# Hybrid encoder block on one Trainium2 core: four stage boundaries reordered, and a PSUM bank for each up product

## Chip, core and metric

The kernel runs on one NeuronCore of a Trainium2 chip. The metric is device time in microseconds from the start to the end of one execution; the time before is 1674.95 us, the median of 3 runs (1673.62 to 1676.17). Engines are named as the profile names them: PE is TensorE, DVE is VectorE, ACT is ScalarE, POOL is GpSimd, SP is the engine whose queue issues the DMAs.

## What is computed

One layer of a hybrid encoder on x of 1024 rows by 1024 columns, all in float32. Cut to what matters here:

```python
h = rmsnorm(x, norm_mix_g)
c_q, c_kv, k_rope, mq, mk, mv, mo, mgates, gate_a, gate_b = split_cols(h @ w_in)
y_attn = mla_branch(c_q, c_kv, k_rope, cos, sin, ...)   # latents c_q, c_kv; rotary tables cos, sin
y_mlstm = mlstm_branch(mq, mk, mv, mo, mgates, ...)
merged = sigmoid(gate_a) * (y_attn @ w_branch_mla) + sigmoid(gate_b) * (y_mlstm @ w_branch_mlstm)
x = x + merged @ w_out
u = rmsnorm(x, norm_mlp_g) @ w_mlp_up                   # 1024 -> 4096
x = x + square(relu(u)) @ w_mlp_down                    # 4096 -> 1024
return rmsnorm(x, norm_final_g)
```

## The kernel before

**Precision by splitting.** Nearly every operand of a product is held as two fp32r tiles, a rounded high part and the rest. `split` (line 77) makes them: a cast on ACT (line 79), then a subtraction on DVE (line 80), which waits for the cast. A product of two operands is three matmuls (high by high, high by low, low by high). Activations scaled in the split go through lines 82 and 83.

**Buffers.** All working tiles of 4 KB a partition come from one pool of 46 slots. Raw weights come from a second pool of 4 (`wr`). PSUM has two double banks (`bankA`) and four single ones (`bankB`). A tile waits until a buffer of its pool is free, which is when the last reader of an earlier tile is done.

**What sets the order.** The program is unrolled and traced. A planner of the tile framework then gives each engine its own list of instructions: it goes by modelled durations, takes what is ready and has a buffer, and prefers what comes earlier in the program. On the chip each engine's list runs in that order, with semaphores between the engines. DMA issues stand in SP's list in the same way.

**Gate b and the latents.** `gate_b` (line 823) has eight steps. Step m takes 128 gate columns (`w_ga`, prefetched one entry ahead), a tanh on ACT (line 829), a scaling on DVE (line 830), then 128 columns of the mLSTM branch product, multiplies the two on DVE (line 836) and stores the result. At its end it calls `down_sums` (line 794): two 512 KB loads of down weights, four DVE operations (lines 801 to 804), two 512 KB stores. Those sums serve the down product much later. After gate b come `rotary` (line 396: angle steps on DVE, lines 407 to 419, one Sin on ACT, line 420, copies on DVE) and `latents` (line 857), whose first act is `w_la.get("cq")`. That fetches the query latent's weights in four chunks of 128x768, and the next three chunks as well, and splits them. `Stream.fetch(upto)` (line 114) loads and splits the entries up to a given one that are not yet split.

**Up.** The up product is done in 16 pairs of 128-column blocks with Strassen-like sums: seven products of 512 columns a pair, each of 12 matmuls (`product`, line 1160). They are named by their two operands: 11x11, 12x21, S2xT2, S3xT3, S1xT1, 22xT4, S4x22. `Pair.load` requests raw up weights (line 1122), `plain` splits the block for "11" and "12", `sums`, `sums_14` and `plain_22` make the rest. The right-hand operands T1 to T4 and 22 are made once, by `minus` (line 1288) and `parts` (line 1281), in the stretch between the output product and `up_pair`. In that same stretch the first two products of pairs 0 to 4 are done early (`first_products`, line 1172; its copies to SBUF on ACT are lines 1177 and 1179). `up_pair` (line 1197) does the other five of those pairs, and all seven of pairs 5 to 15. `add` (line 1198) adds a bank to an SBUF tile on DVE. In `up_pair`, before the change, bank `b1` holds 11x11 plus 12x21; `b2` accumulates S2xT2, then S3xT3, then 22xT4, and is read by an `add` after each; `b3` accumulates S1xT1, then S4x22. After its products `activate` runs relu and square on ACT (lines 1184, 1185), and `keep` does four more DVE operations (lines 1190 to 1193) and stores seven 256 KB tiles to DRAM (`hid_d`).

**Down.** `operands(p, ph)` (line 1350) loads and splits two pairs of tiles of up pair p for phase ph: hidden tiles and down weights, 512 KB each, through the four `wr` buffers (line 1334), casts at line 79 and subtractions at line 80 as `dh` and `dl`. The first group of the down product takes operands of pairs 0 to 3, one pair after the other (`dmul`, line 1370; matmuls at lines 1376 to 1378); the next phase's operands are requested after the first half of the products.

Of the kernel before, what the change touches and what calls it, by code (L numbers as in the profile page):

```python
# [38 lines left out]
def kernel(ctx: ExitStack, tc: tile.TileContext, x, positions, norm_mix_g, w_in, mla_q_norm_g,  # L39
# [16 lines left out]
    def nm(p):  # L56
        cnt[0] += 1
        return f"{p}{cnt[0]}"

    def slot(shape, dt=F32, p="s"):  # L60
        return sl.tile(shape, dt, tag="s", name=nm(p))
# [4 lines left out]
    def bankA(p="a"):  # L66
        return psa.tile([P, 1024], F32, tag="A", name=nm(p))

    def bankB(p="b"):
        return psb.tile([P, 512], F32, tag="B", name=nm(p))  # L70
# [16 lines left out]
    class Stream:  # L87
# [5 lines left out]
        def add(self, key, w, cols, K):  # L93

            N = sum(n for _, n in cols)
            per = max(1, 1024 // N)
            for k0 in range(0, K // P, per):
                kn = min(per, K // P - k0)
                self.plan.append((key, [w[k0 * P:(k0 + kn) * P, c:c + n] for c, n in cols], kn, N))
            self.where[key] = len(self.plan)  # L100
# [137 lines left out]
    w_ml, w_ga, w_la, w_at, w_mg = Stream(2), Stream(1), Stream(3), Stream(0), Stream()  # L238
# [555 lines left out]
    def down_sums(p):  # L794

        y, z = slot([P, 2, 512], F32, "wy"), slot([P, 2, 512], F32, "wz")
        rows = w_mlp_down[0][2 * p * P:(2 * p + 2) * P, :].rearrange("(j p) n -> p j n", p=P)
        nc.sync.dma_start(out=y, in_=rows[:, :, 0:512])
        nc.sync.dma_start(out=z, in_=rows[:, :, 512:1024])
        a, b = slot([P, 2, 512], F32, "wt"), slot([P, 2, 512], F32, "wt")  # L800
        nc.vector.tensor_tensor(out=b[:, 1], in0=z[:, 0], in1=y[:, 0], op=ALU.subtract)
        nc.vector.tensor_tensor(out=a[:, 0], in0=z[:, 1], in1=b[:, 1], op=ALU.subtract)
        nc.vector.tensor_tensor(out=a[:, 1], in0=z[:, 1], in1=z[:, 0], op=ALU.subtract)
        nc.vector.tensor_tensor(out=b[:, 0], in0=y[:, 1], in1=a[:, 0], op=ALU.subtract)
        nc.sync.dma_start(out=wd_d[p][:, 0:2, :], in_=a)
        nc.sync.dma_start(out=wd_d[p][:, 2:4, :], in_=b)

    summed = list(range(DFF // P // 2))
# [14 lines left out]
    def gate_b():  # L823
        for m in range(8):
            wt = w_ga.get(("gb", m))
            pa = bankA()
            yield from tr_mm(pa, xT, wt)
            s = slot([P, 1024], F32, "sg")
            nc.scalar.activation(out=s, in_=pa, func=AF.Tanh, scale=0.5)
            nc.vector.tensor_scalar(out=s, in0=s, scalar1=0.5, scalar2=0.5, op0=ALU.mult, op1=ALU.add)  # L830
            if m == 0:
                yield from flip_y()
            wt = w_ga.get(("wb", m))
            pa = bankA()
            yield from tr_mm(pa, yT_tr, wt)
            nc.vector.tensor_tensor(out=s, in0=pa, in1=s, op=ALU.mult)
            dt_ = dr.tile([P, 1024], F32, tag="brb", name=nm("db"), bufs=8)
            nc.sync.dma_start(out=dt_, in_=s)
            brb.append(dt_)
            dump("brb", s, lambda o, m=m: o[m])  # L840
            down_sums(summed.pop(0))


    up = {}
# [308 lines left out]
    NP = DFF // P // 2  # L1153
    pairs = [Pair(p) for p in range(NP)]
# [5 lines left out]
    def product(o, p, a, b, first):  # L1160

        ah, al = pairs[p].ops[a]
        for k in range(4):
            bh, bl = B[b][k // 2]
            bh, bl = bh[:, k % 2], bl[:, k % 2]
            for i, (x_, y_) in enumerate(((ah, bh), (ah, bl), (al, bh))):
                nc.tensor.matmul(out=o, lhsT=x_[:, k], rhs=y_, start=(first and k == 0 and i == 0),  # L1167
                                 stop=(k == 3 and i == 2), skip_group_check=True)
# [28 lines left out]
    def up_pair(p):  # L1197
        add = lambda o, x_, y_: nc.vector.tensor_tensor(out=o, in0=x_, in1=y_, op=ALU.add)
        nx = pairs[p + 1] if p + 1 < NP else None
        if p + 2 < NP:  # L1200
            pairs[p + 2].load()
        r0, b1 = early.pop(p, None), None
        if r0 is None:
            b1 = bankB()
            r0 = slot([P, 2, 512], F32, "r")
            product(b1, p, "11", "11", True)
            nc.scalar.copy(out=r0[:, 1], in_=b1)
        m1 = r0[:, 1]
        u = slot([P, 2, 512], F32, "u")
        b2 = bankB()  # L1210
        product(b2, p, "S2", "T2", True)
        add(u[:, 0], b2, m1)
        if b1 is not None:
            product(b1, p, "12", "21", False)
            nc.scalar.copy(out=r0[:, 0], in_=b1)
        if nx and p + 1 >= EARLY:
            nx.plain()
        product(b2, p, "S3", "T3", False)
        add(u[:, 1], b2, m1)
        if nx:  # L1220
            nx.sums()
        r1 = slot([P, 2, 512], F32, "r")
        b3 = bankB()
        product(b3, p, "S1", "T1", True)
        add(r1[:, 1], b3, u[:, 1])
        if nx:
            nx.plain_22()
        product(b2, p, "22", "T4", False)
        add(r1[:, 0], b2, m1)
        activate(r1)  # L1230
        if nx:
            nx.sums_14()
        product(b3, p, "S4", "22", False)
        add(r0[:, 1], b3, u[:, 0])
        activate(r0)
        keep(p, r0, r1, u)
        pairs[p] = None
# [12 lines left out]
    for half in range(2):  # L1250
        xs = []
        for j in range(4):
            t = half * 4 + j
            xx = slot([P, 1024], F32, "xm")
            nc.sync.dma_start(out=xx, in_=x[0, t * P:(t + 1) * P, :])
            pa = bankA()
            for n in range(2):
                nat_mm(pa[:, n * 512:(n + 1) * 512], mg, t, wo[n])
            nc.vector.tensor_tensor(out=xx, in0=pa, in1=xx, op=ALU.add)
            dump("xmid", xx, lambda o, t=t: o[t])  # L1260
            nc.sync.dma_start(out=xmd[t], in_=xx)
            xs.append(xx)
            if half == 1 and j in (1, 3):
                pairs[j // 2].load(1)
                pairs[j // 2].plain()
        for q in range(4):
            f = slot([P, 2, 512], F32, "xf")
            for i in range(2):
                k = 2 * q + i
                pb = bankB()  # L1270
                for j in range(4):
                    nc.tensor.transpose(out=pb[:, j * P:(j + 1) * P], in_=xs[j][:, k * P:(k + 1) * P], identity=ident)
                nc.scalar.activation(out=f[:, i], in_=pb, func=AF.Copy, scale=vec("gmlp", k))
            blk[q // 2, half, q % 2] = f
            if half == 0:
                h, l = slot([P, 2, 512], F32R, "bh"), slot([P, 2, 512], F32R, "bl")
                split(h, l, f)
                B.setdefault(f"{q // 2 + 1}1", []).append((h, l))
        if half == 0:
            squares(half, xs)  # L1280
# [9 lines left out]


    t1 = [minus(blk[0, 1, q], blk[0, 0, q]) for q in range(2)]
    pairs[2].load(1)
    pairs[2].plain()
    t2 = [minus(blk[1, 1, q], t1[q]) for q in range(2)]
    for q in range(2):
        parts("T2", t2[q])
    pairs[0].load()
    for p in range(2):
        early[p] = first_products(p)  # L1300
    pairs[0].sums()
# [1 line left out]
    pairs[0].sums_14()  # L1303
    for q in range(2):
        parts("T3", minus(blk[1, 1, q], blk[0, 1, q]))
    pairs[3].load(1)
    pairs[3].plain()
    early[2] = first_products(2)
    for q in range(2):
        parts("T1", t1[q])  # L1310
    pairs[4].load(1)
    pairs[4].plain()
    early[3] = first_products(3)
    for q in range(2):
# [4 lines left out]
    squares(1, xs)  # L1319
    nc.vector.tensor_scalar(out=rsq, in0=msq, scalar1=EPS, scalar2=None, op0=ALU.add)  # L1320
    nc.vector.reciprocal(out=rsq, in_=rsq)


    pairs[1].load()
    for p in range(NP):
        up_pair(p)


    GD = 4

# [6 lines left out]
    def in_pair(srcs):  # L1337
        r = raw_pair(srcs)
        h, l = slot([P, 2, 512], F32R, "dh"), slot([P, 2, 512], F32R, "dl")
        split(h, l, r)  # L1340
        return [(h[:, j], l[:, j]) for j in range(2)]
# [8 lines left out]
    def operands(p, ph):  # L1350

        if ph == 3:
            return in_last(p)
        right = ([down_row(p, 0)[:, 0:512], down_row(p, 1)[:, 0:512]] if ph == 0 else
                 [wd_d[p][:, 2 * (ph - 1) + j, :] for j in range(2)])
        return [in_pair([hid_d[p][:, 2 * ph + j, :] for j in range(2)]), in_pair(right)]

    acc = {}

# [42 lines left out]
                                       op0=ALU.mult, op1=ALU.add)  # L1402

    NG = NP // GD
    nxt = [operands(p, 0) for p in range(GD)]
    xm = [None] * 8
    every = range(GD)
    for g in range(NG):
# [22 lines left out]
        nxt = [operands(p, 1) for p in group]  # L1431
# [15 lines left out]
        nxt = [operands(p, 2) for p in group]  # L1447
# [5 lines left out]
        if not last:  # L1453
# [9 lines left out]
            nxt = [operands(p + GD, 0) for p in group]  # L1463
# [41 lines left out]
```

## Time and profile before

| What | us |
|---|---|
| median of 3 runs | 1674.95 |
| the profiled execution | 1676.88 |
| its span, first to last instruction | 1675.1 |
| PE busy | 1614.1 |
| DVE busy | 1051.5 |
| ACT busy | 745.0 |

A row of the timeline gives the start and the length in us, the engine, the line of the kernel, the operation, the tile written and the tiles read, shapes and count; in square brackets stands how long the engine had been idle before it and what ended that. A row of the table by stretches gives the stretch, its length, then the busy time of PE, of the weight loads (PEld), of DVE, ACT and POOL with their instruction counts, then the granted share of PE's clock, the busy share of the DMA engines and the GB/s moved. A full clock is 2.4 GHz, a share of 0.50 is 1.2 GHz.

### The profile page before, as it was taken

The numbers are of one execution on the slowest core, as the hardware profiler recorded it, in microseconds if no ns is written. First come the engines' busy times: TensorE is split into PE (matmuls) and PEld (weight loads), VectorE is DVE, ScalarE is ACT, GpSimd is POOL, SyncE is SP. The second block draws the span as 40 slices with busy tenths as digits, with TensorE's granted clock in tenths as the row PEclk, the third lists the DMA queues.
The fourth block names the chain that finished last, engine by engine and source line by source line (L and its number), as shares of the span: only waits on it lengthen the run. The fifth ranks groups of instructions, "written<-read, shape, count | busy, mean of one in ns | idle before, by whom it ended". The sixth has DMA issues, their size and how long they took to land.

```text
span 1675.1 us, 22459 instructions
## 1 busy us (share of the span) xinstructions
PE 1614.1 (96%) x8421; PEld 1358.4 (81%) x8421; DVE 1051.5 (63%) x1551; ACT 745.0 (44%) x1275; POOL 196.0 (12%) x363
## 2 busy tenths in 40 slices
PE   7999999999998999999999998999999989999997
PEld 6789888888887988989888886778888868888885
DVE  5686857665334257787887226666666456666695
ACT  6254444432112267676763125544444356333342
POOL 4021120200000343334310000000000000000001
PEclk9999999999998999999999998999999999999999
DMA  7122220366563000000026532454444377655752
GB/s 217 50 77 64 85 92 14 107 232 204 191 216 123 14 1 14 2 13 1 7 70 251 164 102 76 138 176 170 139 151 140 125 245 246 210 182 192 252 188 101
DMA packets 160528, 211.03 MB, mean 126 GB/s; under 512 B 10835, under 2 KB 93732, under 8 KB 160420
## 3 DMA queue, kind: packets, MB, share of 16 engines
q1 hardware_dynamic: 160388, 209.60, 37.5%
q8 instruction: 66, 1.08, 0.3%
q14 instruction: 42, 0.34, 0.1%
q10 hardware_dynamic: 32, 0.01, 0.0%
HBM read 146.65 MB, written 62.91 MB: 125 GB/s over the span
## 4 chain that ended last, share of the span: by engine, by line
PE 86%; DVE 5%; ACT 3%; issue 3%; POOL 1%; DMA 1%; SPq 0%; POOLq 0%; ACTq 0%; DVEq 0%
PE b L1167 17%; PE a L232 7%; PE a L228 7%; PE a L227 7%; PE a L204 5%; PE a L205 5%; PE a L206 5%; PE b L1007 3%; PE a L1377 3%; PE a L1378 3%; PE a L1376 3%; PE b L1377 2%; PE b L1376 2%; PE b L1378 2%; PE a L986 2%
## 5 line engine op out<-in xcount | busy, mean ns | idle before, releaser
L227 PE MATMUL a<-th,wh 128*128 128x512 f32 x504 | 201.4, 400 | 0.0
L228 PE MATMUL a<-tl,wh 128*128 128x512 f32 x504 | 201.4, 400 | 0.0
L79 ACT CAST dh<-wr 128x1024 fp32r<-128x1024 f32 x112 | 114.2, 1049 | 157.3 <-PE a L1377 49.0
L80 DVE TENSOR_TENSOR dl<-wr,dh 128x1024 fp32r<-128x1024 f32 x112 | 134.1, 1221 | 62.0 <-ACT dh L79 61.3
L1167 PE MATMUL b<-bh,wh 128*128 128x512 f32 x384 | 151.2, 399 | 11.6 <-ACT wh L79 7.1
L232 PE MATMUL a<-th,wl 128*128 128x512 f32 x504 | 162.2, 399 | 0.0
L204 PE MATMUL a<-wh,th 128*128 128x256 f32 (+5 forms) x504 | 161.6, 321 | 0.2 <-ACT mo L569 0.2
L205 PE MATMUL a<-wl,th 128*128 128x256 f32 (+5 forms) x504 | 160.5, 319 | 0.3 <-DVE wl L80 0.3
L206 PE MATMUL a<-wh,tl 128*128 128x256 f32 (+5 forms) x504 | 160.5, 319 | 0.0
L1167 PE MATMUL b<-bl,wh 128*128 128x512 f32 x384 | 152.2, 396 | 0.0
L1167 PE MATMUL b<-bh,wl 128*128 128x512 f32 x384 | 150.7, 396 | 0.0
L306 POOL TENSOR_SCALAR m<-m 128x1 f32<-128x1 f32 (+1 forms) x40 | 9.8, 245 | 1093.1 <-ACT o L1383 802.5
L227 PEld LDWEIGHTS a<-th,wh 128*128 128x128 f32 x504 | 94.7, 188 | 20.6 <-issue 0.2
L228 PEld LDWEIGHTS a<-tl,wh 128*128 128x128 f32 x504 | 94.7, 188 | 20.4
L232 PEld LDWEIGHTS a<-th,wl 128*128 128x128 f32 x504 | 94.0, 188 | 20.8
L1377 PE MATMUL a<-dl,dh 128*128 128x512 f32 x256 | 101.9, 398 | 2.7 <-DVE dl L80 2.7
L80 DVE TENSOR_TENSOR wl<-wr,wh 128x1024 fp32r<-128x1024 f32 (+6 forms) x86 | 93.2, 1096 | 15.8 <-ACT wh L79 11.8
L1378 PE MATMUL a<-dh,dl 128*128 128x512 f32 x256 | 101.5, 397 | 0.0
L204 PEld LDWEIGHTS a<-wh,th 128*128 128x128 f32 x504 | 95.2, 189 | 6.7 <-ACT P L993 0.5
L205 PEld LDWEIGHTS a<-wl,th 128*128 128x128 f32 x504 | 95.2, 189 | 6.4 <-DVE wl L80 0.8
L206 PEld LDWEIGHTS a<-wh,tl 128*128 128x128 f32 x504 | 95.1, 189 | 5.4
L1167 PEld LDWEIGHTS b<-bh,wh 128*128 128x128 f32 x384 | 72.7, 189 | 31.8 <-ACT wh L79 8.5
(310 smaller groups left out, 3727.0 us busy)
## 6 DMA issues: line engine op xcount, KB each, us to landing
wr<-hid SPq DMA_DIRECT2D x112, 256.0 KB, 3.9
wr<-in_w_mlp_up SPq DMA_DIRECT2D x37, 512.0 KB, 4.0
wdd<-wt SPq DMA_DIRECT2D x32, 512.0 KB, 3.1
hid<-r SPq DMA_DIRECT2D x64, 256.0 KB, 2.1
wr<-wdd SPq DMA_DIRECT2D x64, 256.0 KB, 4.4
wr<-in_w_in SPq DMA_DIRECT2D x24, 512.0 KB, 3.8
wr<-in_w_mlp_down SPq DMA_DIRECT2D x48, 256.0 KB, 2.7
wy<-in_w_mlp_down SPq DMA_DIRECT2D x16, 512.0 KB, 5.6
```

Source lines behind the costliest of these rows:

```text
L79: nc.scalar.copy(out=h, in_=src)
L80: (eng or nc.vector).tensor_tensor(out=l, in0=src, in1=h.bitcast(F32), op=ALU.subtract)
L204: nc.tensor.matmul(out=ps, lhsT=xh, rhs=wh, start=(k == 0), stop=False)
L205: nc.tensor.matmul(out=ps, lhsT=xh, rhs=wl, start=False, stop=False)
L206: nc.tensor.matmul(out=ps, lhsT=xl, rhs=wh, start=False, stop=(k == n - 1))
L227: nc.tensor.matmul(out=o, lhsT=wts[k][0], rhs=xh, start=(k == 0), stop=False)
L228: nc.tensor.matmul(out=o, lhsT=wts[k][0], rhs=xl, start=False, stop=False)
L232: nc.tensor.matmul(out=o, lhsT=wts[k][1], rhs=xh, start=False, stop=(k == n - 1))
L1167: nc.tensor.matmul(out=o, lhsT=x_[:, k], rhs=y_, start=(first and k == 0 and i == 0), stop=(k == 3 and i == 2), skip_group_check=True)
L1376: nc.tensor.matmul(out=o, lhsT=ah[:, c], rhs=bh, start=st, stop=False, skip_group_check=True)
L1377: nc.tensor.matmul(out=o, lhsT=ah[:, c], rhs=bl, start=False, stop=False, skip_group_check=True)
L1378: nc.tensor.matmul(out=o, lhsT=al[:, c], rhs=bh, start=False, stop=en, skip_group_check=True)
```

## The change

Four places are edited; what is computed stays the same.

1. In `gate_b` the down-weight sums are made two at a time in steps 1 and 3, one at a time in steps 0, 2, 4 and 5, and not in steps 6 and 7. At the end of step 6 the four chunks of the query latent's weights are fetched, which loads and splits them.
2. Before the up pairs: the raw weights of pairs 2 and 3 are requested at the end of the output product, the split of pair 3 comes before the first products of pairs 0 and 1, and the load of pair 4 comes where pair 3's was.
3. In `up_pair` S3xT3 and 22xT4 each get a bank of their own. The additions on DVE take the sum so far from SBUF in place of the accumulation in PSUM.
4. In the last up pair the operands of down pairs 0 and 1 are requested and split behind the S1xT1 product; those of pairs 2 and 3 stay behind the up pairs. For that the helper functions of the down product move above the loop over the pairs.

```diff
@@ gate_b
-            down_sums(summed.pop(0))
+            for _ in range(2 if m in (1, 3) else 1 if m < 6 else 0):
+                down_sums(summed.pop(0))
+            if m == 6:
+                w_la.fetch(4)
@@ up_pair
-        product(b2, p, "S3", "T3", False)
-        add(u[:, 1], b2, m1)
+        b2 = bankB()
+        product(b2, p, "S3", "T3", True)
+        add(u[:, 1], b2, u[:, 0])
...
         product(b3, p, "S1", "T1", True)
+        if p == NP - 1:
+            nxt.extend(operands(i, 0) for i in range(2))
         add(r1[:, 1], b3, u[:, 1])
...
-        product(b2, p, "22", "T4", False)
-        add(r1[:, 0], b2, m1)
+        b2 = bankB()
+        product(b2, p, "22", "T4", True)
+        add(r1[:, 0], b2, u[:, 1])
@@ between the output product and the up pairs
             if half == 1 and j in (1, 3):
                 pairs[j // 2].load(1)
                 pairs[j // 2].plain()
+            if half == 1 and j == 3:
+                pairs[2].load(1)
+                pairs[3].load(1)
...
 t1 = [minus(blk[0, 1, q], blk[0, 0, q]) for q in range(2)]
-    pairs[2].load(1)
 pairs[2].plain()
...
 pairs[0].load()
+    pairs[3].plain()
 for p in range(2):
     early[p] = first_products(p)
...
-    pairs[3].load(1)
-    pairs[3].plain()
+    pairs[4].load(1)
 early[2] = first_products(2)
...
-    pairs[4].load(1)
 pairs[4].plain()
...
+    nxt = []
 for p in range(NP):
     up_pair(p)
...
-    nxt = [operands(p, 0) for p in range(GD)]
+    nxt += [operands(p, 0) for p in range(2, GD)]
```

## Rows read from the trace of the kernel before

**Rows 1.** The page's first part: busy time, share of the span, instructions.

```profile
PE 1614.1 (96%) x8421; PEld 1358.4 (81%) x8421; DVE 1051.5 (63%) x1551; ACT 745.0 (44%) x1275; POOL 196.0 (12%) x363
```

**Rows 2.** Timeline of PE: the first matmul behind each of its waits.

```profile
516.98 1.33 PE L204 MATMUL b<-wh,th 128*128 128x384 f32 x3 [7.58 <-ACT wh L79]
...
1032.32 1.28 PE L1167 MATMUL b<-bh,wh 128*128 128x512 f32 x2 [7.13 <-ACT wh L79]
...
1069.77 0.50 PE L1167 MATMUL b<-bh,wh 128*128 128x512 f32 x1 [1.13 <-DVE u L1198]
...
1344.90 1.09 PE L1376 MATMUL a<-dh,dh 128*128 128x512 f32 x2 [4.84 <-ACT dh L79]
1347.94 0.80 PE L1377 MATMUL a<-dl,dh 128*128 128x512 f32 x1 [1.96 <-DVE dl L80]
```

**Rows 3.** Table by stretches: behind three waits, one up pair, one gate step.

```profile
516.98:522.50 5.52, 5.52 (x17) 5.34 (x18) 3.62 (x5) 3.06 (x4) 0.00 (x0) 0.50 0.62 193
...
1032.30:1037.90 5.60, 5.58 (x13) 4.33 (x14) 5.58 (x6) 3.29 (x4) 0.00 (x0) 0.50 0.33 94
1347.90:1351.90 4.00, 3.96 (x9) 3.17 (x10) 2.92 (x3) 1.04 (x1) 0.00 (x0) 0.50 0.82 246
1085.60:1101.50 15.90, 14.55 (x60) 11.05 (x60) 11.14 (x17) 6.75 (x7) 0.00 (x0) 1.00 0.54 182
466.60:483.25 16.65, 16.65 (x73) 13.51 (x73) 6.16 (x8) 2.48 (x3) 0.52 (x16) 1.00 0.57 198
```

**Rows 4.** Timeline of DVE, ACT and SP between gate b and the latents.

```profile
515.47 0.29 DVE L419 TENSOR_SCALAR s<-s 128x256 f32<-128x256 f32 x1
...
515.79 0.42 ACT L420 ACTIVATE rot<-s 128x256 f32<-128x256 f32 x1 [9.56 <-DVE s L419]
516.12 3.02 ACT L79 CAST wh<-wr 128x768 fp32r<-128x768 f32 x4
...
497.42 1.64 SPq L110 DMA_DIRECT2D wr<-in_w_in  x1
```

**Rows 5.** Timeline of DVE: the last two weight splits of gate b.

```profile
489.24 1.23 DVE L80 TENSOR_TENSOR wl<-wr,wh 128x1024 fp32r<-128x1024 f32 x1 [0.24 <-ACT wh L79]
...
495.70 0.68 DVE L80 TENSOR_TENSOR wl<-wr,wh 128x512 fp32r<-128x512 f32 x1
```

**Rows 6.** The page's DMA issues: count, KB each, median us to landing.

```profile
wr<-in_w_in SPq DMA_DIRECT2D x24, 512.0 KB, 3.8
```

**Rows 7.** Waits, whole span: engine, line, releaser, total us, times, longest.

```profile
DVE wt L801 <- DMA wz<-in_w_mlp_down: 9.0, 3, 4.5
```

**Rows 8.** Timeline of DVE and ACT before the up pairs.

```profile
1025.56 1.22 DVE L1288 TENSOR_TENSOR xt<-xf,xf 128x1024 f32<-128x1024 f32 x1
...
1031.23 1.04 ACT L79 CAST wh<-wr 128x1024 fp32r<-128x1024 f32 x1
1032.18 0.58 ACT L1177 COPY r<-b 128x512 f32<-128x512 f32 x1
```

**Rows 9.** Timeline of DVE between up pairs 0 and 1.

```profile
1063.59 0.69 DVE L1198 TENSOR_TENSOR r<-b,u 128x512 f32<-128x512 f32 x1 [1.84 <-PE b L1167]
1066.50 0.69 DVE L1190 TENSOR_TENSOR u<-r,r 128x512 f32<-128x512 f32 x1 [2.22 <-ACT r L1185]
...
1069.03 0.68 DVE L1198 TENSOR_TENSOR u<-b,r 128x512 f32<-128x512 f32 x1
```

**Rows 10.** Chain that ended last, merged: pairs 4 to 15 (start, us, what).

```profile
1117.37 222.70 PE b L1167 x960
```

**Rows 11.** Timeline of ACT and SP between up and down.

```profile
1338.04 1.06 ACT L1184 ACTIVATE r<-r 128x1024 f32<-128x1024 f32 x1 [8.23 <-DVE r L1198]
1342.87 3.87 ACT L79 CAST dh<-wr 128x1024 fp32r<-128x1024 f32 x4
1350.17 1.04 ACT L79 CAST dh<-wr 128x1024 fp32r<-128x1024 f32 x1 [3.43 <-DMA wr<-hid]
...
1316.46 0.81 SPq L1334 DMA_DIRECT2D wr<-in_w_mlp_down  x2
```

More of the change, by code (lines that the diff above doesn't have):

```diff
@@ L1321 @@
     nc.vector.reciprocal(out=rsq, in_=rsq)
-    pairs[1].load()
-    for p in range(NP):
-        up_pair(p)
     GD = 4
@@ L1356, in operands @@
         return [in_pair([hid_d[p][:, 2 * ph + j, :] for j in range(2)]), in_pair(right)]
+    pairs[1].load()
+    nxt = []
+    for p in range(NP):
+        up_pair(p)
     acc = {}
```

## The prediction

> **What bounds the kernel now.** I read the page's engine shares first: TensorE (PE) is busy 96% of the span [rows 1]. So an edit pays only where it takes away PE idleness or a stretch in which PE runs at the half clock. I then went through PE's timeline for its waits behind the first 30 us. The long ones stand at the four places that the diff touches [rows 2]: 7.58 us before the first latent product (a cast on ACT ends it), 7.13 us before the up products of pair 3 (again a cast), 1.13 us inside each of pairs 1 to 4 (a DVE addition; one row of four, the others are 1.10 to 1.14), and 4.84 and 1.96 us before the down products (a cast, then the subtraction behind it). Third, the table by stretches shows the clock [rows 3]: after each of the three long waits the granted share is 0.50, that is 1.2 GHz instead of 2.4, for 5.52, 5.58 and 3.96 us of PE work, half of which is lost. After the 1.13 us waits it stays at 1.00.
>
> **Latent weights ahead of the rotary tables.** PE stands still because ACT's queue holds the four latent casts at 516.12 behind the Sin of the rotary table, which waited 9.56 us for DVE's angle steps, the last at 515.47. The weights had long been requested, the last chunk at 497.42 [rows 4]. The change puts the casts and subtractions of all four chunks into the seventh step of gate b. ACT works there 2.48 us of 16.65 and DVE 6.16 [rows 3], so 4 casts of 0.75 (3.02/4) and 4 subtractions of about 0.9 fit beside PE. What would be late next? Not ACT, which still reaches the first square only after Sin at 516.2: 17 matmuls in 5.52 us at half clock are 0.16 each at full clock, a tile of 24 takes 3.9 us, and four banks give PE 15.6 us before it needs a reader. So the 7.58 us go, and with them the half-clock loss of 5.52/2 = 2.76: **10.3 us**.
>
> Two costs stand against this. First, the four latent chunks now stand in the four-buffer weight ring ahead of the last branch weights, whose split ended at 496.4 [rows 5], about 7.5 us before PE began them (24 matmuls of 0.23 before the end at 509.4). Their load must now wait for a latent chunk's subtraction on DVE. If that runs only after the addition at 492.8, the weights are ready around 500 (0.9 subtraction, 3.8 load [rows 6], 1.4 split), so some 4 us are left: nothing. Second, the down-weight sums are doubled in steps 1 and 3. Each adds four DVE operations (2.5 us, so 8.7 of 16.65) and 2 MB to the 3.3 MB that a step moves at 198 GB/s, or 320 GB/s in these two steps. If a load lags, DVE waits in L801 with the next weight split queued behind it. Earlier in the kernel it did so three times, 4.5 us at most [rows 7]. The gate split ends at 490.5 [rows 5], 2.2 us before PE needs it, so the price is 0 to 2 x 2.3 = 4.6 us. I take 0, since loads run a step ahead. Range of this part: 5.7 to 10.3.
>
> **Up weights sooner.** At 1025.2 PE has done "11" of pairs 0 to 2 and "12" of pairs 0 and 1. It then needs pair 3's weights, cast at 1031.23, and "12" of pair 2 needs ACT's copy of its first half, which runs at 1032.18. Both stand in ACT's queue behind the casts of T3, whose first subtraction DVE starts at 1025.56 [rows 8]. Pair 3's cast now comes ahead of pair 0's sums. "11" of pair 3 (12 x 0.232 = 2.78 us) then fills 1025.2 to 1028.0. The copy of pair 2 still stands behind T3, which slips by the 1.2 us of the moved subtraction: to about 1032.4, PE again at 1033.0. That leaves a 5 us gap instead of 7.1, but four products behind it instead of five. The last "12" now ends at 1032.3 + 5 x 2.78 + 2.79 = 1049.0. After the change it is 1033.0 + 4 x 2.78 + 0.3 = 1044.4 if the clock stays, 1047.2 if it falls as now: 1.8 to 4.6 gained. If the copy gets ahead of the T3 casts, all 7.13 + 2.79 = 9.9 can go. I take **4**, near the walk, with 1.8 to 9.9 kept. The load of pair 4 moves too, but its buffer comes free at the same moment (pair 2's subtraction), so it costs nothing. Pair 3's own load moves in the ring ahead of pair 0's two and was long landed: nothing.
>
> **A bank for each up product.** In pairs 0 to 4 PE waits because S3xT3 accumulates into the bank that DVE has still to read, and that addition stands on DVE behind the previous pair's last four operations, which wait 2.22 us for ACT's two activations: addition at 1069.03, 5.4 us after the previous pair's last addition [rows 9]. With 60 matmuls in 15.9 us [rows 3] against 960 in 222.70 [rows 10], or 13.9 per 60, a pair loses 1.95; four such pairs lose 7.8 us. With a bank of its own S3xT3 need not wait. Next late is the last product, which still accumulates on S1xT1's bank. DVE must read that first, and in its queue the read stands behind the sums of the next pair. From one pair's last addition to the next's: 0.7 addition, 2.2 activations, 2.5 for four operations, 1.2 for two additions, 1.8 for three sums, 1.05 cast, 1.2 subtraction, 0.65 read, 2.78 product, an estimated 0.3 of hand-overs: 14.4 us, against PE's 13.9. So 1.45 of 1.95 is gained, four times: **5.8 us**; bounds 3 (half as much) and 7.8. In pairs 5 to 15 PE runs without a gap today [rows 10], so nothing is gained there. Five products now share four banks; the fifth takes the bank of the second, read about 7 us before, so it costs nothing as long as PE keeps program order.
>
> **First down operands sooner.** ACT is idle 8.23 us before 1338.04 while the operands of pairs 0 and 1, requested by 1316.46, wait to be cast at 1342.87 [rows 11]. Cast in that gap, 4 x 0.97 us, they let PE go on when the last up product ends. Costs: their four subtractions (1.2 each) stand on DVE ahead of the read of S1xT1's bank, so the last product starts up to 0.9 later. Pairs 2 and 3 follow only after the last activation (1343) and the last four DVE operations 2.5 us later, while PE ends pairs 0 and 1 by about 1346.5: some 2 us of wait. Loads of the next phase are bounded by four weight buffers; ACT waits for them 3.43 us at 1350.17 [rows 11], so I leave another 1.5. Lost now: 4.84 + 1.96, half of 3.96, half of 1.09 [rows 2, 3], 9.3 in all. Gain 9.3 - 4.4 = **5 us**, bounds 0 and 9.3.
>
> **The sum.** 10.3 + 4 + 5.8 + 5 = 25.1 us. The profiled execution took 1676.88 us, of which 1675.1 is the span; 1676.9 - 25.1 = 1651.8. It lay 1.9 above the median of the runs, so 1650 for the median.
>
> **The rivals.** *The planner keeps the old order.* Each engine's order is set at build by a planner that goes by modelled times and free buffers, not by program order alone. If the up and down casts stay where they are, and the pairs gain only 3: 10.3 + 3, so 1674.95 - 13.3 = 1661.7. For it: ACT idled at 1330 with the operands already requested and nothing was pulled forward. Against it: the planner does follow program order among work that is ready.
>
> *Everything goes.* 10.3 + 9.9 + 7.8 + 9.3 = 37.3: 1637.7. Against it: DVE's chain at the up start and in the pairs.
>
> *The ring of banks bites.* If the planner lets PE take a bank early, the products of pairs 5 to 15 find none free until DVE has done the addition that ends 6.1 us after the previous pair's last product [rows 9]. With one product as cover that is 6.1 - 2.8 = 3.3 us in 11 pairs, 36 us, and the pairs 1 to 4 gain nothing: 1674.95 - 19.3 + 36.3 = 1692. It decides from 19.3/11 = 1.75 us a pair on. Against it: those pairs run gapless with three banks today and each extra bank is free some 7 us before it is wanted. The Trainium skill, "TensorE: Matmul & The Clock Gate", section "A second HAM failure mode: psum-queue depth-cycling", tells of a kernel that moves through its banks each iteration, idles briefly between groups and so has its clock swing. By that rule the up pairs would lose clock as well; the trace does not agree so far, since pairs 1 to 4 have such short waits at a clock of 1.00 [rows 3].
>
> **How the numbers follow.** Forecast 0.58, planner keeps its order 0.20, everything goes 0.12, nothing measurable 0.04, ring of banks 0.06. Low end: everything goes, 1638. High end: the planner's case with 2 us of lagging loads in gate b, 1664. A difference under 0.2% (3.4 us) can't be told from no change here. Faster 0.90, same 0.04, slower 0.06.
>
> **What would show it.** Latents: their casts before the rotary Sin, no wait at 509, clock 1.00 after it. Up start: pair 3's cast before pair 0's copies, one gap of about 5 us. Pairs 1 to 4: about 14.4 us each. Pairs 5 to 15: still 0.232 a matmul. Down start: four casts before 1338, short waits behind pairs 0 and 1. The forecast is wrong if gate b gets PE gaps, if the casts don't move, or if gaps come back in the down phases because loads can't keep up.

## The result

The changed kernel took 1652.3 us, the median of 4 runs (1652.09 to 1653.19), beside 1674.43 us for the kernel before (4 runs, 1673.62 to 1676.17): a ratio of 0.9867, interval 0.985 to 0.9885. The forecast was 1650. The profiled executions differ by 24.55 us (1676.88 and 1652.33; spans 1675.1 and 1650.5), where the forecast's sum was 25.1.

The page's first part for the changed kernel answers to [rows 1]: PE's busy time fell by 6.9 us, the rest of the gain is waits that are gone.

```profile
PE 1607.2 (97%) x8421; PEld 1354.8 (82%) x8421; DVE 1051.5 (64%) x1551; ACT 744.2 (45%) x1275; POOL 195.6 (12%) x363
```

The next fence is the timeline of PE in the changed kernel: the first matmul behind each wait at the four places, and the first latent matmul.

```profile
422.12 0.74 PE L232 MATMUL a<-th,wl 128*128 128x512 f32 x2 [1.07 <-DVE wl L80]
...
456.95 0.72 PE L232 MATMUL a<-th,wl 128*128 128x512 f32 x2 [1.20 <-DVE wl L80]
...
511.68 0.34 PE L204 MATMUL b<-wh,th 128*128 128x384 f32 x1
...
1024.96 0.79 PE L1170 MATMUL b<-bh,wh 128*128 128x512 f32 x1 [4.95 <-ACT r L1180]
...
1331.36 0.50 PE L1386 MATMUL a<-dl,dh 128*128 128x512 f32 x1 [1.90 <-DVE dl L80]
```

Against [rows 2]: the waits of 7.58 us (latents), 1.13 us (pairs) and 4.84 us (down) are gone, 7.13 us at the up start became 4.95, and the 1.96 us inside down all but stayed (1.90). Two waits in gate b, at 422.12 and 456.95, are new. The table by stretches (stretch, length, busy time of PE, PEld, DVE, ACT, POOL, clock share, DMA share, GB/s) answers to [rows 3]. The trace has the granted share at 0.50 in two stretches only: from 1023.18 to 1030.01 at the up start, and in the last 6 us.

```profile
511.70:517.20 5.50, 5.50 (x33) 5.50 (x32) 4.30 (x7) 1.77 (x4) 0.31 (x2) 1.00 0.48 160
1025.00:1030.60 5.60, 5.60 (x14) 4.41 (x15) 5.31 (x5) 3.48 (x5) 0.00 (x0) 0.55 0.01 3
1331.40:1335.40 4.00, 4.00 (x17) 3.26 (x18) 2.17 (x2) 0.03 (x1) 0.00 (x0) 1.00 0.77 247
1038.50:1066.00 27.50, 27.50 (x121) 22.35 (x120) 20.11 (x31) 14.70 (x20) 0.00 (x0) 1.00 0.38 126
```

To place the gain I took the start of one matmul per stage from PE's timeline of both kernels (up and down matmuls are counted from their first; 120 of them are the early products):

| Point | before | after | difference | gained since the point above |
|---|---|---|---|---|
| PE begins the gates (first L227) | 47.47 | 47.05 | -0.42 | 0.42 |
| gate b ends | 509.40 | 511.84 | +2.44 | -2.86 |
| scores begin | 605.18 | 597.36 | -7.82 | 10.26 |
| up begins | 1011.05 | 1003.02 | -8.03 | 0.21 |
| up matmul 120 | 1048.89 | 1038.49 | -10.40 | 2.37 |
| last up matmul ends | 1340.06 | 1323.46 | -16.60 | 6.20 |
| down matmul 48 | 1361.87 | 1336.56 | -25.31 | 8.71 |
| span ends | 1675.07 | 1650.51 | -24.56 | -0.75 |

So latents 10.26 less 2.86 paid in gate b, up start 2.4, banks 6.2, down 8.7 less 0.75 paid behind its matmul 48. The readings that follow show the mechanisms.

**Latents.** Timeline of ACT: the latents' four casts now run 14 to 20 us ahead of the Sin at 510.28, where in [rows 4] they stood behind it.

```profile
490.56 3.24 ACT L79 CAST wh<-wr 128x1024 fp32r<-128x1024 f32 x4
...
510.28 0.42 ACT L420 ACTIVATE rot<-s 128x256 f32<-128x256 f32 x1 [1.63 <-DVE s L419]
```

(The group of four mixes one gate cast with three latent ones; the fourth is at 496.15.)

**Gate b.** Timeline of SP and DVE in step 1, and behind it the row of the waits over the whole span, where [rows 7] had 9.0 us in three times.

```profile
410.29 0.34 SPq L838 DMA_DIRECT2D db<-sg  x1
...
412.09 0.34 SPq L805 DMA_DIRECT2D wdd<-wt  x1
412.82 0.34 SPq L806 DMA_DIRECT2D wdd<-wt  x1
413.25 0.94 SPq L799 DMA_DIRECT2D wz<-in_w_mlp_down  x1
...
419.57 0.69 DVE L801 TENSOR_TENSOR wt<-wz,wy 128x512 f32<-128x512 f32 x1 [6.78 <-DMA wz<-in_w_mlp_down]
...
421.38 0.68 DVE L80 TENSOR_TENSOR wl<-wr,wh 128x512 fp32r<-128x512 f32 x1
```

```profile
DVE wt L801 <- DMA wz<-in_w_mlp_down: 23.5, 6, 6.9
```

The second sum of a doubled step asks for its wz behind the step's store and both stores of the first sum, on the same SP queue. DVE waits for it with the weight split queued behind, and PE waits for the split. The chain that ended last (start, us, what) now runs through both loads:

```profile
413.25 6.22 DMA wz<-in_w_mlp_down
447.91 6.36 DMA wz<-in_w_mlp_down
...
1024.96 42.83 PE b L1170 x174
...
1077.46 1.24 DVE wl L80
1078.74 3.74 PE b L1170 x15
...
1092.16 1.24 DVE wl L80
1093.44 230.03 PE b L1170 x992
```

**Pairs.** In the third row above 174 up matmuls are one unbroken piece of the chain, where before every one of these pairs broke it. In pairs 2 and 3 the chain still goes through DVE: a weight split at 1077.46 and one at 1092.16 let PE go on. But PE waits there for 0.18 us at most. DVE's last addition of pairs 0 to 2 shows that its loop is indeed longer than PE's 13.9 us, 15.24 and 14.70 from one to the next (the first holds some 0.7 us in which the bank had been read and PE was still at other products):

```profile
1052.57 0.69 DVE L1201 TENSOR_TENSOR r<-b,u 128x512 f32<-128x512 f32 x1 [1.69 <-PE b L1170]
...
1067.81 0.69 DVE L1201 TENSOR_TENSOR r<-b,u 128x512 f32<-128x512 f32 x1 [1.37 <-PE b L1170]
...
1082.51 0.69 DVE L1201 TENSOR_TENSOR r<-b,u 128x512 f32<-128x512 f32 x1 [0.89 <-PE b L1170]
```

PE is hardly held by it: between the first two of these rows it began 66 matmuls, not 60, so it takes the next pair's products ahead of the last one of this pair. Over these few pairs that suffices.

**Down.** Timeline of ACT: the casts of pairs 0 and 1 (three and one) fill the wait for the last sums; those of pairs 2 and 3 follow the activations at 1326.28, and PE's wait of 1.90 us is the wait for the splits behind them. Compare [rows 11].

```profile
1307.35 2.95 ACT L79 CAST dh<-wr 128x1024 fp32r<-128x1024 f32 x3
...
1313.13 1.05 ACT L79 CAST dh<-wr 128x1024 fp32r<-128x1024 f32 x1
1321.45 1.06 ACT L1187 ACTIVATE r<-r 128x1024 f32<-128x1024 f32 x1 [7.27 <-DVE r L1201]
...
1326.28 3.87 ACT L79 CAST dh<-wr 128x1024 fp32r<-128x1024 f32 x4
```

Behind matmul 48 the change loses 0.75 us again. Timeline of PE, the waits that follow there in the changed kernel (two) and in the kernel before (one), and the loads through which the changed kernel's chain comes to its two:

```profile
1350.68 0.73 PE L1385 MATMUL b<-dh,dh 128*128 128x512 f32 x2 [0.63 <-ACT dh L79]
...
1371.96 0.50 PE L1385 MATMUL b<-dh,dh 128*128 128x512 f32 x1 [0.55 <-ACT acc L1375]
```

```profile
1376.08 0.73 PE L1376 MATMUL b<-dh,dh 128*128 128x512 f32 x2 [0.74 <-ACT dh L79]
```

```profile
1343.78 5.77 DMA wr<-wdd
...
1363.00 5.92 DMA wr<-hid
```

### The profile page after: what moved, and what is told of

Same layout as the page of the kernel before. It is cut to its first block, busy times and chain, and to the rows that moved or that the text cites. A ratio compares the mean times of both kernels' runs of the same rounds, so it can differ in the third digit from the quotient of the medians.

```text
span 1650.5 us, 22439 instructions
## 1 busy us (share of the span) xinstructions
PE 1607.2 (97%) x8421; PEld 1354.8 (82%) x8421; DVE 1051.5 (64%) x1551; ACT 744.2 (45%) x1275; POOL 195.6 (12%) x363
## 4 chain that ended last, share of the span: by engine, by line
PE 84%; DVE 6%; issue 3%; ACT 3%; DMA 2%; POOL 1%; SPq 0%; POOLq 0%; DVEq 0%; ACTq 0%
PE b L1170 17%; PE a L232 7%; PE a L228 6%; PE a L227 6%; PE a L204 5%; PE a L205 5%; PE a L206 5%; PE b L1010 3%; PE a L1386 3%; PE a L1385 3%; PE a L1387 3%; PE b L1386 2%; PE b L1387 2%; PE b L1385 2%; PE a L989 2%
## 5 line engine op out<-in xcount | busy, mean ns | idle before, releaser
L227 PE MATMUL a<-th,wh 128*128 128x512 f32 x504 | 201.3, 399 | 0.0
L227 PEld LDWEIGHTS a<-th,wh 128*128 128x128 f32 x504 | 94.7, 188 | 20.6 <-issue 0.2
L996 ACT ACTIVATE P<-a,m 128x1024 f32<-128x1024 f32 x64 | 71.5, 1118 | 55.3 <-DVE m L994 49.0
```

The costliest lines, as they stand in the source:

```text
L227: nc.tensor.matmul(out=o, lhsT=wts[k][0], rhs=xh, start=(k == 0), stop=False)
```

## The experiments

Each kernel was timed in rounds beside the kernel before on the same chip, so ratios are compared; those of one chip share their runs of before. Theory: the four parts lie in different stages and add, each by the mechanism of the forecast. Rivals stand with each.

### Each part alone

**e1_latents**: before, with part 1 alone.

```diff
-            down_sums(summed.pop(0))
+            for _ in range(2 if m in (1, 3) else 1 if m < 6 else 0):
+                down_sums(summed.pop(0))
+            if m == 6:
+                w_la.fetch(4)
```

> The kernel before with part 1 alone (the latents' weights split in gate b, the down-weight sums doubled in steps 1 and 3). Theory: the parts act each in its own stage and add up. Then the 7.58 us wait before the latents and its half-clock stretch (2.76 us) go, two PE waits of about 1.1 us come back in gate b where DVE waits for the doubled sums' loads, and the span falls by 7 to 8 us against the kernel before (1675.1). Rival: the earlier latents only bring the same wait back in front of the up products, because the later stages are set by loads or by DVE: then under 3 us of gain.

1669.47 us, ratio 0.996 (0.9948 to 0.9973). PE's 7.6 us wait at the latents is gone; gate b has waits of 1.95 and 1.61 us that end in the weight split, as in the whole change. The later stages keep theirs (7.08, 4.84, 1.83). The part does on its own what it does in the change.

**e2_upstart**: before, with part 2 alone.

```diff
+                pairs[2].load(1)
+                pairs[3].load(1)
...
-    pairs[2].load(1)
...
+    pairs[3].plain()
     for p in range(2):
         early[p] = first_products(p)
```

> The kernel before with part 2 alone (pair 3's split ahead of pair 0's sums, loads moved). Theory: one product fills part of the wait, so the 7.13 us wait becomes about 5 and the clock still falls behind it: 2 to 2.5 us of gain. Rival: the walk of the prediction, that the shorter wait spares the clock or that the copy moves forward: 4 us or more.

1675.45 us, ratio 0.9995 (0.9986 to 1.0004): no gain, which neither side expected. The wait at the up start did shrink to 5.04 us, and the early products ended 2.5 us earlier. But PE's timeline and the stretch behind it show where that went:

```profile
1068.01 0.50 PE L1167 MATMUL b<-bh,wh 128*128 128x512 f32 x1 [1.81 <-DVE u L1198]
...
1085.45 0.50 PE L1167 MATMUL b<-bh,wh 128*128 128x512 f32 x1 [1.13 <-DVE u L1198]
```

```profile
1068.50:1071.80 3.30, 3.30 (x10) 2.53 (x9) 1.94 (x4) 1.96 (x3) 0.00 (x0) 0.50 0.20 75
```

The wait between pairs 0 and 1 grew from 1.13 to 1.81 us and a stretch at half clock followed it; the last up matmul ended at 1339.99, as before (1340.06). The two causes can be told apart by the same two waits of the kernel before, the first of which ended at 1069.77 [rows 2], and the second here:

```profile
1085.63 0.50 PE L1167 MATMUL b<-bh,wh 128*128 128x512 f32 x1 [1.10 <-DVE u L1198]
```

Behind the first of them PE was still 1.76 us ahead of the kernel before, behind the second 0.18: the wait at the shared bank took 0.8 of the 2.5 us, the half clock 1.6. From the first up matmul to the last the stage took 329.0 us before and here, 322.4 with part 3 alone (e3) and 320.4 with all parts, so part 2 kept some 2 us where part 3 had taken that wait away. This rests on profiled executions; the interval here does not exclude a gain of up to 2.3 us.

**e3_banks**: before, with part 3 alone.

```diff
+        b2 = bankB()
-        product(b2, p, "S3", "T3", False)
+        product(b2, p, "S3", "T3", True)
-        add(u[:, 1], b2, m1)
+        add(u[:, 1], b2, u[:, 0])
```

(and the same for 22xT4)

> The kernel before with part 3 alone (a bank each for S3xT3 and 22xT4). Theory: the four waits of 1.1 us and the short ones behind them go, pairs 0 to 4 run at 0.232 us a matmul, 6 to 6.5 us of gain. Rival: pairs 1 to 4 stay limited by DVE's chain at 14.4 us a pair and the gain in the changed kernel came from the earlier start: 3 us or less here. Pairs 5 to 15 unchanged in both.

1669.42 us, ratio 0.9962 (0.9949 to 0.9976). The up stage is 6.65 us shorter, and no wait of a microsecond is left between its pairs. Theory held.

**e4_down**: before, with part 4 alone.

```diff
+        if p == NP - 1:
+            nxt.extend(operands(i, 0) for i in range(2))
...
-    nxt = [operands(p, 0) for p in range(GD)]
+    nxt += [operands(p, 0) for p in range(2, GD)]
```

> The kernel before with part 4 alone (operands of down pairs 0 and 1 split in the last up pair). Theory: the 4.84 us wait and the half-clock stretch behind it go, one wait of about 1.9 stays, 8 to 8.5 us of gain at the first down products, kept to the end. Rival of the prediction: the last up product starts 0.9 late and the next phase waits 1.5 longer for loads, so 5 us.

1668.36 us, ratio 0.9956 (0.9943 to 0.9968). The 4.84 us wait is gone; 1.89 us remain, with 3.41 us at half clock behind it. The four medians gain 6.2, 0.2, 6.3 and 7.3, together 20.0 of the 22.1 of the whole. The missing 2 are of the size of the up start's gain, which e2 lost; but each of these medians is uncertain by about as much, so the sum alone doesn't prove it.

### What makes gate b longer, and what brings the latents forward

**e5_sums_later**: one sum a step, the last two inside the latents.

```diff
-            for _ in range(2 if m in (1, 3) else 1 if m < 6 else 0):
+            if m < 6:
                 down_sums(summed.pop(0))
...
             if key == "ckv":
                 w_at.fetch(2)
+                for _ in range(2):
+                    down_sums(summed.pop(0))
```

> The changed kernel, with one down-weight sum in each of gate b's steps 0 to 5 and the last two moved into the latents. Theory: the doubled sums cost 2.9 us in gate b, because DVE waits 6.8 us for the second load with a branch weight's split queued behind it; without them both PE waits (1.07 and 1.20) go and the span falls by 2.5 to 3 us against the changed kernel. Rival: the branch weights are late because the latents' chunks stand ahead of them in the ring of four raw buffers; then the two waits stay. In the latents DVE is little used, so the two sums cost nothing there.

1656.08 us, ratio 0.9886 (0.9871 to 0.99): no gain over the change, if anything a loss (the intervals touch). Gate b has no waits and ends at 509.16, so the doubled sums are their cause. But the same wait moved (timeline of SP, DVE and PE):

```profile
549.88 0.34 SPq L806 DMA_DIRECT2D wdd<-wt  x1
550.31 0.82 SPq L799 DMA_DIRECT2D wz<-in_w_mlp_down  x1
...
556.42 0.69 DVE L801 TENSOR_TENSOR wt<-wz,wy 128x512 f32<-128x512 f32 x1 [6.57 <-DMA wz<-in_w_mlp_down]
...
558.77 0.66 PE L867 MATMUL b<-identr,c 128*128 128x128 f32 x4 [4.03 <-DVE c L896]
```

There the latents' normalisation (L896) stands behind it, with less cover: 4.03 us and a stretch at half clock instead of two short waits.

**e6_no_fetch**: the change without its fetch.

```diff
-            if m == 6:
-                w_la.fetch(4)
```

> The changed kernel without the early fetch of the latents' weights; the sums stay doubled. Theory: the fetch is what moves the casts ahead of the rotary Sin; without it the wait of about 7 us and the half clock behind it come back and the span grows by 8 to 10 us. Rival: steps 6 and 7 without sums leave slots and DVE time, so that the planner pulls the casts forward by itself; then under 2 us.

1656.18 us, ratio 0.9888 (0.9873 to 0.9903). My theory fell, the rival was nearly right. Without the fetch the wait at the latents is only 1.95 us, and the clock stays (timeline of DVE and PE):

```profile
510.51 0.30 DVE L419 TENSOR_SCALAR s<-s 128x256 f32<-128x256 f32 x1
...
515.04 0.45 PE L205 MATMUL b<-wl,th 128*128 128x384 f32 x1 [1.95 <-DVE wl L80]
```

With no sums in steps 6 and 7 the rotary's steps on DVE move up into gate b: the last one ran at 510.51, 4.5 us ahead of the matmul behind the wait, and no longer at 515.47, 1.5 us ahead of it [rows 2, 4]. The casts still stand behind the Sin (at 511.16), but a weight split ends the wait now. From the end of gate b to the scores it takes 95.8 us before, 87.9 here and 85.5 in the change. So 7.9 of the 10.3 us come from clearing DVE of sums, and the fetch adds 2.4 to that. What the fetch would bring with the sums left where they were was not run.

**e9_one_double**: one doubled step, the last sum in step 6.

```diff
-            for _ in range(2 if m in (1, 3) else 1 if m < 6 else 0):
+            for _ in range(2 if m == 1 else 1 if m < 7 else 0):
```

> The changed kernel with one doubled sum (step 1 of gate b) in place of two, and one sum in each of steps 0 and 2 to 6, so that the last sum stands two steps ahead of the latents and not three. Theory: each doubled sum costs a wait of PE of 1.1 to 1.9 us (the second sum's load is late and a weight split stands behind it on DVE), so one of the two gaps (421.05 1.07 and 455.75 1.20 in the changed kernel) goes and the other stays: gate b 1.1 to 1.5 us shorter, the latents' first product without a wait, and the whole 1 to 1.5 us below the changed kernel. Rival: the last sum's two loads and two stores, now in step 6, push the loads of the latents' weights back on SP, and a wait of about 2 us or more stands ahead of the latents again: 0 to 3 us slower than the changed kernel.

1651.94 us, ratio 0.9854 (0.9838 to 0.9871), which can't be told from the change's 0.9867. One wait stays (1.20 us, up to 422.47), the other is gone, gate b ends 1.1 us earlier, and the latents start without a wait. In the profiled execution that was lost again at the scores: behind the same 1.4 us wait as ever (1.44, 1.43 in the changed kernel) the clock fell here and not there:

```profile
606.10:612.90 6.80, 6.79 (x19) 5.35 (x20) 4.04 (x7) 3.57 (x8) 2.24 (x2) 0.50 0.00 0
```

**e11_loads_first**: both sums' loads ahead of the first sum's work (`down_sums` cut in two).

```diff
-            for _ in range(2 if m in (1, 3) else 1 if m < 6 else 0):
-                down_sums(summed.pop(0))
+            n = 2 if m in (1, 3) else 1 if m < 6 else 0
+            for w in [down_loads(summed.pop(0)) for _ in range(n)]:
+                down_sums(*w)
```

> The changed kernel with both sums' loads of a doubled step issued ahead of the first sum's DVE operations and stores. In the changed kernel the second wz load was issued at 413.25, behind the store of the step's branch (410.29) and both stores of the first sum (412.09, 412.82), and DVE waited 6.78 us for it with a weight split behind it. Theory: the wait for wz shrinks by 3 us or more in both doubled steps, PE's gaps of 1.07 and 1.20 go, gate b ends 2 to 2.9 us earlier, and the time is 2 to 3 us below the changed kernel. Rival: the next weights' load now stands behind the stores (it was issued at 406.76, ahead of them) and comes some 8 us later, and PE waits for that in place of the split: 0 to 4 us slower than the changed kernel.

1650.02 us, ratio 0.9846 (0.9831 to 0.9861). Theory held in the trace. DVE goes from the first sum to the second without a wait, and the split comes 6.7 us earlier than at 421.38 (timeline of DVE):

```profile
412.88 0.68 DVE L804 TENSOR_TENSOR wt<-wz,wy 128x512 f32<-128x512 f32 x1
...
414.68 0.68 DVE L80 TENSOR_TENSOR wl<-wr,wh 128x512 fp32r<-128x512 f32 x1
```

Gate b ends at 509.17, 2.7 us earlier. The next weights' load did move behind the stores (issued at 416.40 instead of 406.76), as the rival said, but was still in time. By the time alone neither this run nor e10 below can be told from the change, since the intervals overlap; that they gain rests on their traces and on e12.

### What is left at up and down

**e7_p4_first**: pair 4's split and the first products of pairs 2 and 3 ahead of pair 0's sums and T3.

```diff
+    pairs[4].load(1)
     for p in range(2):
         early[p] = first_products(p)
+    pairs[4].plain()
+    for p in range(2, 4):
+        early[p] = first_products(p)
     pairs[0].sums()
```

(the lines that did this further down are taken out)

> The changed kernel, with the load and split of pair 4 and the first products of pairs 2 and 3 ahead of pair 0's sums and of T3. Theory: the 4.95 us wait stands there because ACT's copy of pair 2's first half queues behind the T3 casts; with the copies and pair 4's cast ahead of them the wait and the half clock go, 4 to 7 us of gain. Rival: DVE's chain of sums and T operands is the bound; then the wait comes back before S2xT2 or S3xT3 of pair 0 and the gain is under 2 us.

1659.23 us, ratio 0.9902 (0.9888 to 0.9917), slower than the change: the rival was nearly right. The early products run without a wait, but the sums' split on DVE waits 7.02 us for a cast that now stands behind copies. DVE's work behind it is late: its first sum for pair 1 starts at 1048.17, in the changed kernel at 1042.15. So PE's wait comes back later and longer, not ahead of pair 0's products as the rival said but ahead of pair 1's (timeline of DVE and PE):

```profile
1025.83 1.23 DVE L80 TENSOR_TENSOR wl<-ws,wh 128x1024 fp32r<-128x1024 f32 x1 [7.02 <-ACT wh L79]
...
1048.17 0.68 DVE L1138 TENSOR_TENSOR ws<-wr 128x512 f32<-128x512 f32 x1
...
1053.44 0.79 PE L1170 MATMUL b<-bh,wh 128*128 128x512 f32 x1 [6.58 <-ACT wh L79]
```

So the 4.95 us are not a matter of the copy's place alone: ACT's and DVE's work on sums and T operands bounds this stage.

**e8_one_bank**: an own bank for S3xT3 only.

```diff
-        b2 = bankB()
-        product(b2, p, "22", "T4", True)
-        add(r1[:, 0], b2, u[:, 1])
+        product(b2, p, "22", "T4", False)
+        add(r1[:, 0], b2, u[:, 0])
```

> The changed kernel with a bank of its own for S3xT3 alone; 22xT4 accumulates on that bank again. Theory: the waits came from S3xT3's bank, so nearly all of the 6.2 us stays gained; 22xT4 may wait 0.2 to 0.6 us in pairs 1 to 4 where it comes right behind S3xT3: 0 to 2.5 us slower than the changed kernel. Rival: both banks are needed, 4 us or more slower.

1654.19 us, ratio 0.9873 (0.9856 to 0.9889), the change's within the interval. From the early products' end to the last up matmul it takes 285.4 us here and 285.0 in the change, with waits of up to 0.68 us between pairs. The bank for S3xT3 carries nearly all of part 3.

**e10_all_operands**: the operands of down pairs 2 and 3 too inside the last up pair, behind the sum that reads S1xT1.

```diff
         add(r1[:, 1], b3, u[:, 1])
+        if p == NP - 1:
+            nxt.extend(operands(i, 0) for i in range(2, GD))
...
-    nxt += [operands(p, 0) for p in range(2, GD)]
```

> The changed kernel with the down operands of pairs 2 and 3 also issued inside the last up pair (behind the sum that reads S1xT1), so that their casts stand ahead of the last pair's activations on ACT and not behind them. Theory: the 1.9 us wait at 1329.46 is ACT's four casts at 1326.28, which stood in its queue behind activations that waited 7.27 us for the last sums, though their loads were issued at 1311.57 to 1315.46; ACT is idle from 1314.2 to 1321.4, so they fit there. The 1.9 us wait goes, perhaps the 0.63 one too: 1.9 to 2.5 us below the changed kernel, and no stretch at half clock behind the start of down. Rival: four more splits on DVE (4.6 us) ahead of the sum that reads 22xT4 hold back the last activations and the stores of the last hidden pair, or the loads land only at 1318 or later, so that the wait stays or moves: within 1 us of the changed kernel.

1650.44 us, ratio 0.9849 (0.9835 to 0.9864). Theory held in the trace: the casts fit ahead of the activations (timeline of ACT, the first and the last of the four), PE goes into down without a wait, and down matmul 48 starts 2.2 us earlier than in the change.

```profile
1316.08 1.05 ACT L79 CAST dh<-wr 128x1024 fp32r<-128x1024 f32 x1 [1.95 <-DMA wr<-hid]
...
1321.49 1.05 ACT L79 CAST dh<-wr 128x1024 fp32r<-128x1024 f32 x1 [0.22 <-DMA wr<-in_w_mlp_down]
```

The activations start 3 us later (1324.44), and nobody waits for them: their pair is wanted by the down product only in its last group.

**e12_both**: e10 and e11 together.

```diff
+            for w in [down_loads(summed.pop(0)) for _ in range(n)]:
+                down_sums(*w)
...
+            nxt.extend(operands(i, 0) for i in range(2, GD))
```

> The changed kernel with both edits that gained: the loads of a doubled sum issued first, and all four pairs' first down operands issued inside the last up pair. They lie in different stages, so the theory is that they add: gate b without a wait of PE (2.7 us shorter than in the changed kernel), no wait at the start of down (1.9 us) and no stretch at half clock behind it, together 4.5 to 5.5 us below the changed kernel, near 1647.5 us, a ratio of some 0.983 to the kernel before. Rival: what one stage gains another gives back, as in the study of the up start alone (a longer stretch at half clock behind the 4.95 us wait at the up start, say): 1649 to 1650 us, no better than either edit alone.

1648.03 us (1646.86 to 1649.93), ratio 0.9833 (0.9819 to 0.9846): the fastest of all, and its interval lies below the change's (0.985 to 0.9885). In the table by stretches gate b's step and the start of down are full:

```profile
421.00:438.80 17.80, 17.80 (x79) 14.46 (x78) 6.84 (x9) 3.63 (x5) 0.00 (x0) 1.00 0.89 299
...
1322.30:1333.40 11.10, 11.10 (x49) 8.92 (x48) 3.75 (x6) 4.92 (x5) 0.00 (x0) 1.00 0.79 288
605.00:611.60 6.60, 6.60 (x21) 5.23 (x21) 3.84 (x7) 3.29 (x6) 2.24 (x2) 0.51 0.01 2
```

The third row is the scores' stretch at half clock, which came here too; so the parts add, less about 2 us that one stage gave back in the profiled execution.

## Why the prediction was right, and where its terms were off

- **The total.** 25.1 us were forecast from the profiled execution, 24.55 came. That it is so close is in part luck: gate b cost 2.9 us that were taken at 0 and the up start gave 1.6 less than its 4, while down gave 3 more than its 5 (8.7 less 0.75) and the banks 0.4 more. The prediction itself had named PE gaps in gate b as a sign that it is wrong, and they came; so did, on a small scale, the waits for loads in the down phases that it named too. The median is 2.3 above the forecast because of the last step: I took 1.9 off since the profiled execution of before lay that much above its median. The changed kernel's profiled execution lies on its own (1652.33 and 1652.3). Such an offset belongs to one execution and should have widened the range, not moved the forecast.
- **Latents, 10.3.** 10.26 came, and PE's first 5.5 us of latents ran at full clock, 33 matmuls against 17 in [rows 3]. But the working credited the moved casts with all of it, and e6 shows that 7.9 come from taking the sums out of steps 6 and 7. What I saw in [rows 4] as DVE's late angle steps was late because the sums stood ahead of them in DVE's queue (the last three operations of a sum ran from 510.58 on, the first angle step behind them at 512.38); I named the wait and not what was queued in front of it.
- **Gate b, taken at 0.** 2.86 was paid, inside the bound of 0 to 4.6; PE's two waits are 2.27 of it, and with them gone (e5, e11) all of it is gone. The mechanism was named rightly (L801 waits, the split stands behind it). The value was wrong because "loads run a step ahead" holds for the first sum of a step only: the second one's wz stands on SP behind the stores of the first. e5 and e11 show it from both sides.
- **Up start, 4.** The wait is 4.95 us, as the walk had it (5), and the clock fell, which the walk priced at 1.8. With 2.4 measured, 4 was too near the upper end of the walk's 1.8 to 4.6, which holds only where the clock stays. That this part can lose its gain at the next stage's shared bank without part 3 (e2) I had not seen: I summed the parts as if each stage handed its gain on.
- **Banks, 5.8.** 6.2 came. The loop on DVE that was to limit PE exists, at 14.7 us (15.2 once, with PE late) instead of my 14.4, but PE works ahead of it. The ring of banks did not bite: pairs 5 to 15 run without a wait, 960 or more matmuls in one piece of the chain. (Not every product has a bank of its own: 12x21 still goes on 11x11's, and S4x22 on S1xT1's.) The Trainium skill ("TensorE: Matmul & The Clock Gate", section "A second HAM failure mode: psum-queue depth-cycling") tells of PE going round the banks and idling briefly between groups of matmuls, so that its clock swings. Here PE went round the banks without idling for more than 0.18 us, and the trace has 27.5 us at a share of 1.00: going round the banks did not by itself cost clock in this kernel.
- **Down, 5.** 8.7 came, near the upper bound of 9.3. Of the three costs I took off (0.9, 2 and 1.5), the 2 us wait for pair 2's operands came in full, and e10 shows that it was ACT's queue, as argued. The 0.9 for a late last product did not come, since the four splits on DVE were done at 1315.4, ahead of the sum at 1317.95 that reads S1xT1. Of the 1.5 for later loads half came: behind matmul 48 stand waits of 0.63 and 0.55 us, where before one of 0.74 stood, and from there to the end the change takes 0.75 us longer. The chain comes to both waits through a load, so loads were the cause, as argued. What the sum of losses left out is a wait of 0.76 us of the kernel before (at 1356.32), which is gone. And the wait of 1.9 us was not followed by half clock in this execution.
- **The rivals.** That the planner keeps the old order is refuted: all three moved groups of casts stand where the program put them (pair 3's at 1010.15, ahead of the copies). That everything goes is refuted by the 4.95 and 1.90 us that stayed.

## What to carry to other kernels

Before pricing a wait, ask what stands in front of the late instruction on its own queue, and what stands in front of the DMA that feeds it: here clearing DVE's queue of the sums gave 7.9 us and moving the late casts forward 2.4 more, and issuing loads ahead of stores took both waits out of gate b. Time gained at a stage's start can be lost again where the next stage waits for another engine, by the longer wait and by the clock behind it; look for that wait first. When work is doubled up in one step, issue all its loads before its first store.

## What the runs showed of the hardware

PE's clock after a wait is not set by the wait's length alone. Granted clock and waits, from the profiled executions of all fourteen kernels: behind the 1.87 to 1.91 us wait at the start of down, where it stood alone, there was no stretch at 1.2 GHz in the changed kernel, e6 and e9, and one of 3.41 us in e4, e5, e7, e8 and e11. Behind the 1.43 to 1.45 us wait at the scores there was none in eleven, 3.41 us in e7, 6.83 us in e9 and e12. Behind the 4.95 to 5.04 us wait at the up start it was 3.41 us in e5, e11 and e12, and 6.83 us in six others. So a shortened wait can give back up to 1.7 or 3.4 us (half of such a stretch) or not, by nothing that these runs show; e9 and e12 lost this way part of what they had gained. What decides it stays open. The Trainium skill ("TensorE: Matmul & The Clock Gate", section "What's actually happening") says that the chip's look at PE's activity runs freely and does not start anew with the kernel; that would fit, and no run here shows it.
